# Weights of a hybrid decoder trunk rounded by the loading DMA, and a second convolution buffer

## The chip, the cores and the metric

The kernel runs on one core of a Trainium2 chip. The metric is the device time of one execution in microseconds (us). The core's engines work side by side: PE (TensorE, the matmuls), DVE (VectorE), ACT (ScalarE), POOL (GpSimd) and SP (SyncE, which here only issues DMAs). A DMA is issued by one engine, whose queue it stands in with that engine's other instructions, and is carried out by the core's DMA engines.

## The reference

Two layers (DEPTH = 2) on x of 1024 tokens by 1024 features, all in float32:

```python
for l in range(DEPTH):
    h = rmsnorm(x, norm_mix[l])
    q, k, v, u, ug, ga, gb = split(h @ w_in[l])          # 1024+128+128+512+512+1024+1024 columns
    A = sliding_window_attention(rope(qknorm(q)), rope(qknorm(k)), v, sinks)   # 16 heads, window 128
    a = u * sigmoid(ug)                                   # 512 channels
    y = causal_depthwise_conv(a, conv_w[l], width=31) + conv_b[l]
    B = silu(layernorm(y, over_channels)) @ w_pw[l]       # 512 -> 1024
    x = x + (sigmoid(ga) * A + sigmoid(gb) * B) @ w_out[l]
    x = x + swiglu(rmsnorm(x, norm_ffn[l]))               # 1024 -> 2816 -> 1024
```

## The kernel before

**Layout.** Features lie on the 128 partitions, the 1024 tokens in the free dimension. So a weight tile has 128 rows of the inner dimension and 128 output columns for each of eight row groups: 128x1024 numbers, 512 KB. The convolution's output weights (`wcv`) have four row groups: 128x512, 256 KB.

**A float32 product is three matmuls.** Each operand is split into a high part, which TensorE's rounded float32 type (F32R) holds exactly, and a low part, what is left: w = wh + wl, x = xh + xl. `mm3` issues wh·xh, wh·xl and wl·xh, each as two matmuls of 512 tokens (profile line L253). So one weight tile is used by 48 matmuls (24 for wcv), and its low part is first read by the fifth of them.

**The weights of one layer, in the order of use.** 34 input projections (`win`: first k and v, then conv value and gate, queries and output gates mixed, the order being a list), 8 wcv, 8 output projections (`wout`). They are 50 a layer, 100 in all; the FFN's weights take another path, which the change leaves alone.

**How weights get ready.** `fetch` runs before each weight's use. It starts the load of the weight two ahead and makes the high and low part of the weight one ahead:
- the load: SP issues a DMA into a raw tile (L128, two tiles);
- the high part: ACT casts raw to wh (L136, three tiles);
- the low part, outside the attention stage: POOL subtracts, wl = raw − wh (L143, two tiles). This is so for k and v, the last win, all wcv and all wout, 38 in the two layers;
- the low part, within the attention stage (flag `spaced`): ACT writes wl = −wh (L146), then POOL issues a DMA that reads the weight from memory once more and adds it into wl as it writes (L147, an accumulating DMA). This is so for 62 weights. Here one spare wl tile more goes round, which has the tag "y", that of the convolution's output.

**The attention stage** (66 to 528 us in layer 0, 1386 to 1848 in layer 1) mixes four streams. PE does the projections and, between them, 32 attention units (scores S, L658; transposes L694; values L724). Between score and transpose stand ACT (copy, exponential L678, scaling L685) and DVE (the mask's copy of S into sc, L670); POOL applies band masks (L706, L709). Queries go through rope (POOL L400, L401), a power (POOL L411), and are stored and reloaded (DMA `qs<-q`). The convolution runs on DVE: four chunks of 128 channels, each 31 taps of 128x1024 (the first L514, the others L518, in place on the chunk's tile y). After a chunk's last tap its y is added into the channel sum lsum (ACT copy for the first, L522; POOL add for the others, L524) and stored to memory (SP, L525, DMA `yd<-y`). When all four are done, matmuls with a matrix of means read lsum (L555) for the layer norm, and the chunks are loaded back.

There is **one** y tile (YB = 1), so the next chunk's first tap waits until the store has read it.

**The output stage** (some 528 to 664 us in layer 0) is wcv, where SP also loads two 512 KB gate tiles for each weight, then wout. In wout the residual (L857), the next norm's squares (ACT L301, POOL sum L303) and the first pieces of FFN weights (ACT cast L160, POOL subtraction L162) run beside the matmuls.

**What sets the order.** The order on PE is written by hand throughout, that on DVE in the attention stage and the FFN. The orders on ACT, POOL and SP come from a scheduler that simulates the program's timeline when it is built, so they move when operations come or go. Every engine works through its instructions strictly in order: one that waits holds up all that stand behind it.

Of the kernel before, what the change touches and what calls it, by code (L numbers as in the profile page):

```python
# [12 lines left out]
F32 = mybir.dt.float32  # L13
F32R = mybir.dt.float32r
U32 = mybir.dt.uint32
AF = mybir.ActivationFunctionType
# [36 lines left out]
def trunk(ctx, tc, xT, win, wcv, wout, wgu, wdn, vecs, cosT, sinT, outT):  # L53
# [15 lines left out]
    dp = pool("dp", 1, DRAM)  # L69
    hlp = wp = psm = None  # L70

# [46 lines left out]
    part = [0]  # L118
    spaced = [False]

    spare = []

    def fetch(limit=len(wseq), parts=len(wseq)):
        limit = min(limit, wends[part[0]])
        while given[2] < limit and given[2] <= given[0] + AHEAD + 1:
            src, n = wseq[given[2]]
            raw = wp.tile([P, n], F32, tag="raw", bufs=WRAW, name="raw")
            nc.sync.dma_start(raw, src)  # L128
            raws.append(raw)
            given[2] += 1  # L130
        while given[1] < min(given[2], parts) and given[1] <= given[0] + AHEAD:
            src, n = wseq[given[1]]
            raw = raws.pop(0)
            wh = wp.tile([P, n], F32R, tag="wh", bufs=WHI, name="wh")
            wl = spare.pop() if spare else wp.tile([P, n], F32R, tag="wl", bufs=WLO, name="wl")
            nc.scalar.copy(wh, raw)  # L136
            low(wl, raw, wh, src)
            ready.append((wh, wl))
            given[1] += 1

    def low(wl, raw, wh, src):
        if not spaced[0]:
            nc.gpsimd.tensor_tensor(out=wl, in0=raw, in1=wh.bitcast(F32), op=ALU.subtract)  # L143
            return

        nc.scalar.activation(wl, wh.bitcast(F32), AF.Copy, scale=-1.0)  # L146
        nc.gpsimd.dma_start(wl, src, accum_op=ALU.add)  # L147

# [180 lines left out]
    for l in range(DEPTH):  # L329
# [174 lines left out]
        def conv_taps():  # L504
# [3 lines left out]
            for c in range(CC):  # L508
# [8 lines left out]
                for j in range(1, CW):  # L517
                    nc.vector.scalar_tensor_tensor(out=y, in0=a[:, j:j + T], scalar=V(w0 + j),  # L518
                                                   in1=y, op0=ALU.mult, op1=ALU.add)
                    if j == CW - 1:  # L520
                        if c == 0:
                            nc.scalar.copy(lsum, y)  # L522
                        else:
                            nc.gpsimd.tensor_tensor(out=lsum, in0=lsum, in1=y, op=ALU.add)  # L524
                        nc.sync.dma_start(yd[c], y)  # L525
# [236 lines left out]
        wk = next_w()  # L762
        spaced[0] = True

# [47 lines left out]
        assert conv_done[0] == CC * CW  # L812
        spaced[0] = False
        dve.close()
# [359 lines left out]
TD, AD = 7.5, 5.5  # L1174
YB = 1
S0 = 16
# [11 lines left out]
QSB = 4  # L1188
WRAW, WHI, WLO, T4 = 2, 3, 2, 4
WD, RD = 2, 0  # L1190
# [63 lines left out]
```

## Time and profile before

Three runs took 2641.04, 2643.77 and 2648.74 us; the median is 2643.77. The profiled execution took 2642.97 us, its span is 2641.3 us.

| | |
|---|---|
| busy time in the span | PE 97%, DVE 67%, POOL 53%, ACT 44% |
| mean granted clock of TensorE | 0.992 |
| hardware DMA queue (issued by SP) | 393.63 MB, 44.4% of the DMA engines' time |
| software DMA queue (issued by POOL) | 32.51 MB, 7.3% |
| PE idle in the attention stages | 26.1 us in layer 0, 27.5 us in layer 1 |
| ACT casts wh (L136) | 100, 98.1 us |
| POOL subtractions wl (L143) | 38, 74.3 us |
| ACT wl = −wh (L146) | 62, 65.4 us |
| POOL issues of accumulating DMAs (L147) | 62, 55.1 us |
| POOL additions of channel sums (L524) | 6, 14.8 us |

Rows of the time order have: start (us from the span's start), duration, engine, line, operation, output<-inputs, and in brackets the idle time just before and what ended it. "x2" joins instructions that follow each other. A wait's releaser is the one that came last by the profile.

### The profile page before, as it was taken

To read this page: it belongs to the slowest core of one execution; us is meant where nothing else is said; L and a number is where in the kernel's file an instruction comes from. 1 tells how busy PE (TensorE), PEld (TensorE's weight loads), DVE (VectorE), ACT (ScalarE), POOL (GpSimd) and SP (SyncE) were. 2 spreads that over 40 slices of the span, in tenths; PEclk is the share of its full clock that TensorE was granted. 3 is DMA by queue.
4 is the path that set the end of the run, shared out by engine and by line. 5 is a ranking of instruction groups with operands and counts; after the bars stand their busy time and mean duration, and the time that the engine had idled before them with its cause. 6 is when DMAs were issued, how large, how long until landed. Compare 5 with 4: busy or idle time off the path is not lost.

```text
span 2641.3 us, 33363 instructions
## 1 busy us (share of the span) xinstructions
PE 2554.7 (97%) x11736; PEld 2089.6 (79%) x11736; DVE 1767.1 (67%) x2063; ACT 1161.9 (44%) x2300; POOL 1398.8 (53%) x996
## 2 busy tenths in 40 slices
PE   8998999999999999999999989999999999999999
PEld 6776877888778888878777778778887788888887
DVE  4788997551677777845636989975517777878344
ACT  5465666622522322344534656666325222233443
POOL 3355665325366776755423556543243667777444
PEclk9999999999999999999999999999999999999999
DMA  5444445673345444576634444457733444446666
GB/s 172 100 114 113 93 112 148 221 257 136 120 159 183 152 159 168 198 256 223 216 93 89 114 114 101 121 132 235 258 119 124 170 169 163 148 168 219 213 225 212
DMA packets 146407, 428.35 MB, mean 162 GB/s; under 512 B 17152, under 2 KB 17408, under 8 KB 146240
## 3 DMA queue, kind: packets, MB, share of 16 engines
q1 hardware_dynamic: 137168, 393.63, 44.4%
q0 software_dynamic: 8928, 32.51, 7.3%
q8 instruction: 92, 1.51, 0.2%
q14 instruction: 75, 0.61, 0.1%
q10 hardware_dynamic: 144, 0.09, 0.0%
HBM read 291.68 MB, written 115.34 MB: 154 GB/s over the span
## 4 chain that ended last, share of the span: by engine, by line
PE 36%; DVE 6%; DMA 3%; ACT 2%; POOL 2%; issue 2%; SPq 0%; DVEq 0%; ACTq 0%; POOLq 0%
PE b L879 23%; PE ps L253 10%; DVE y L518 2%; DMA qs<-q 1%; DMA rot<-q 1%; POOL plo L162 1%; DMA yd<-y 0%; PE po L724 0%; PE psv L253 0%; POOL rot L401 0%; ACT wh L136 0%; PE pT L694 0%; DVE q L415 0%; ACT sc L678 0%; POOL q L400 0%
## 5 line engine op out<-in xcount | busy, mean ns | idle before, releaser
L162 POOL TENSOR_TENSOR plo<-fraw,phi 128x512 fp32r<-128x512 f32 x290 | 425.9, 1477 | 232.5 <-ACT phi L160 220.4
L162 POOL TENSOR_TENSOR plo<-fs,phi 128x512 fp32r<-128x512 f32 x160 | 262.3, 1650 | 252.8 <-ACT phi L160 245.2
L160 ACT CAST phi<-fraw 128x512 fp32r<-128x512 f32 x444 | 257.6, 618 | 236.2 <-POOL plo L162 139.7
L518 DVE SCALAR_TENSOR_TENSOR y<-a,vec,y 128x1024 f32<-128x1024 f32 x240 | 355.2, 1480 | 3.8
L253 PE MATMUL ps<-hx,wh 128*128 128x512 f32 x1056 | 340.1, 403 | 7.2 <-ACT hx L294 7.2
L253 PE MATMUL ps<-lx,wh 128*128 128x512 f32 x1056 | 330.5, 394 | 0.8 <-DVE lx L295 0.8
L160 ACT CAST phi<-fs 128x512 fp32r<-128x512 f32 x160 | 95.5, 620 | 533.9 <-DVE fs L175 533.9
L253 PE MATMUL ps<-hx,wl 128*128 128x512 f32 x1056 | 329.4, 393 | 0.0
L162 DVE TENSOR_TENSOR plo<-fraw,phi 128x512 fp32r<-128x512 f32 x154 | 130.5, 853 | 189.7 <-ACT phi L160 187.5
L879 PE MATMUL b<-plo,phi 128*128 128x512 f32 x616 | 240.6, 391 | 3.9 <-DVE plo L162 3.7
L879 PE MATMUL b<-phi,plo 128*128 128x512 f32 x616 | 239.8, 389 | 0.0
L879 PE MATMUL b<-phi 128*128 128x512 f32 x616 | 239.7, 389 | 0.0
L253 PEld LDWEIGHTS ps<-lx,wh 128*128 128x128 f32 x1056 | 200.7, 190 | 45.8 <-DVE lx L295 1.5
L253 PEld LDWEIGHTS ps<-hx,wl 128*128 128x128 f32 x1056 | 200.0, 189 | 43.3
L253 PEld LDWEIGHTS ps<-hx,wh 128*128 128x128 f32 x1056 | 189.6, 191 | 41.7 <-ACT hx L294 7.2
L678 ACT ACTIVATE sc<-sc,nm,fq 128x129 f32<-128x129 f32 x256 | 123.8, 487 | 120.2 <-DVE nm L676 120.0
L143 POOL TENSOR_TENSOR wl<-raw,wh 128x1024 fp32r<-128x1024 f32 (+1 forms) x38 | 74.3, 1957 | 174.7 <-PE ps L253 134.7
L136 ACT CAST wh<-raw 128x1024 fp32r<-128x1024 f32 (+1 forms) x100 | 98.1, 981 | 152.8 <-PE ps L253 121.5
L147 POOL DMA_DIRECT2D wl<-win x62 | 55.1, 888 | 202.6 <-ACT wl L146 198.6
L943 DVE TENSOR_TENSOR g<-g 128x512 f32<-128x512 f32 x88 | 105.4, 1198 | 65.9 <-POOL g L947 46.2
L709 POOL TENSOR_SCALAR_AFFINE_SELECT ph<-ph 128x512 fp32r<-128x512 f32 x64 | 69.8, 1090 | 143.6 <-DVE pl L701 143.6
L947 POOL TENSOR_TENSOR g<-g,u 128x512 f32<-128x512 f32 (+1 forms) x84 | 128.4, 1546 | 30.2 <-DVE u L1000 23.8
(254 smaller groups left out, 6157.6 us busy)
## 6 DMA issues: line engine op xcount, KB each, us to landing
fraw<-wgu SPq DMA_DIRECT2D x88, 512.0 KB
raw<-win SPq DMA_DIRECT2D x68, 512.0 KB
wl<-win POOLq DMA_DIRECT2D x62, 512.0 KB, 6.5
act<-g SPq DMA_DIRECT2D x44, 512.0 KB
dw<-wdn SPq DMA_DIRECT2D x44, 512.0 KB
td<-g SPq DMA_DIRECT2D x44, 512.0 KB
sd<-dw SPq DMA_DIRECT2D x44, 512.0 KB
fraw<-sd SPq DMA_DIRECT2D x88, 256.0 KB
```

The lines of the kernel that those rows point to most:

```text
L136: nc.scalar.copy(wh, raw)
L143: nc.gpsimd.tensor_tensor(out=wl, in0=raw, in1=wh.bitcast(F32), op=ALU.subtract)
L147: nc.gpsimd.dma_start(wl, src, accum_op=ALU.add)
L160: nc.scalar.copy(hi, src)
L162: (eng or nc.gpsimd).tensor_tensor(out=lo, in0=src, in1=hi.bitcast(F32), op=ALU.subtract)
L253: nc.tensor.matmul(ps[:, sl], a[:, wc], b[:, sl], start=first and j == 0, stop=last and j == 2)
L518: nc.vector.scalar_tensor_tensor(out=y, in0=a[:, j:j + T], scalar=V(w0 + j), in1=y, op0=ALU.mult, op1=ALU.add)
L678: nc.scalar.activation(sc[:, n], sc[:, n], AF.Exp, bias=nm[:, n:n + 1], scale=fq[:, 4 * j + n:4 * j + n + 1], accum_out=den[:, n:n + 1])
L709: nc.gpsimd.affine_select(out=src, in_=src.bitcast(F32), pattern=[[0, 4], [-1, P]], compare_op=ALU.is_gt, fill=0.0, base=0, channel_multip ...
L879: nc.tensor.matmul(ps, w[:, ai * P:(ai + 1) * P], x, start=first and j == 0, stop=last and j == 2, skip_group_check=True)
L943: nc.vector.tensor_tensor(out=o, in0=x, in1=y, op=ALU.subtract)
L947: nc.gpsimd.tensor_tensor(out=g[:, sl], in0=g[:, sl], in1=u[:, sl], op=ALU.mult)
```

## The change

Three edits:

1. From the third weight on, there is no raw tile. The load is issued by POOL, straight into the wh tile, with a conversion from F32 to F32R in the DMA (L132 of the changed kernel). It is still started two weights ahead; since it lands in one of the three wh tiles, it waits until PE has finished the weight three before. The low part is always made the second way: ACT wl = −wh, then an accumulating DMA from POOL. So of 100 ACT casts 2 are left, of 38 POOL subtractions 2, ACT's negations become 98 (82 of 128x1024, 16 of 128x512), POOL's accumulating weight DMAs 98, and 98 loads move from SP to POOL. The first two weights of layer 0 keep raw tiles, in a pool of their own.
2. There are two y tiles (YB = 2).
3. A chunk's addition into the channel sum (six in all) is an accumulating DMA issued by POOL, in place of a POOL addition.

```diff
         while given[2] < limit and given[2] <= given[0] + AHEAD + 1:
             src, n = wseq[given[2]]
-            raw = wp.tile([P, n], F32, tag="raw", bufs=WRAW, name="raw")
-            nc.sync.dma_start(raw, src)
+            if given[2] < 2:
+                raw = ip.tile([P, n], F32, name=f"raw{given[2]}")
+                nc.sync.dma_start(raw, src)
+            else:
+
+                raw = wp.tile([P, n], F32R, tag="wh", bufs=WHI, name="wh")
+                nc.gpsimd.dma_start(raw, src)
             raws.append(raw)
...
             raw = raws.pop(0)
-            wh = wp.tile([P, n], F32R, tag="wh", bufs=WHI, name="wh")
             wl = spare.pop() if spare else wp.tile([P, n], F32R, tag="wl", bufs=WLO, name="wl")
-            nc.scalar.copy(wh, raw)
-            low(wl, raw, wh, src)
+            if given[1] < 2:
+                wh = wp.tile([P, n], F32R, tag="wh", bufs=WHI, name="wh")
+                nc.scalar.copy(wh, raw)
+                nc.gpsimd.tensor_tensor(out=wl, in0=raw, in1=wh.bitcast(F32), op=ALU.subtract)
+            else:
+
+                wh = raw
+                nc.scalar.activation(wl, wh.bitcast(F32), AF.Copy, scale=-1.0)
+                nc.gpsimd.dma_start(wl, src, accum_op=ALU.add)
             ready.append((wh, wl))
...
                         if c == 0:
                             nc.scalar.copy(lsum, y)
                         else:
-                            nc.gpsimd.tensor_tensor(out=lsum, in0=lsum, in1=y, op=ALU.add)
+                            nc.gpsimd.dma_start(lsum, y, accum_op=ALU.add)
                         nc.sync.dma_start(yd[c], y)
...
-YB = 1
+YB = 2
...
-WRAW, WHI, WLO, T4 = 2, 3, 2, 4
+WHI, WLO, T4 = 3, 2, 4
```

The scheduler's orders move with it; PE's stays as it is. POOL's order from the end of the attention stage through wcv into wout (layer 0), before; L162 are FFN pieces, L303 the sum of squares:

```order
L143 TENSOR_TENSOR wl<-raw,wh 128x1024
L143 TENSOR_TENSOR wl<-raw,wh 128x512 x8
L143 TENSOR_TENSOR wl<-raw,wh 128x1024 x3
L162 TENSOR_TENSOR plo<-fraw,phi 128x512 x4
L143 TENSOR_TENSOR wl<-raw,wh 128x1024
L303 TENSOR_TENSOR acc<-acc,sq 128x1024
L162 TENSOR_TENSOR plo<-fraw,phi 128x512 x3
L143 TENSOR_TENSOR wl<-raw,wh 128x1024
```

POOL's order at the same place after, from the load of the third wout (lines are two further down in the changed kernel, L164 is L162 before, L305 is L303):

```order
L132 DMA wh<-wout 128x1024
L147 DMA wl<-wout 128x1024
L132 DMA wh<-wout 128x1024
L147 DMA wl<-wout 128x1024
L164 TENSOR_TENSOR plo<-fraw,phi 128x512 x4
L132 DMA wh<-wout 128x1024
L305 TENSOR_TENSOR acc<-acc,sq 128x1024
L164 TENSOR_TENSOR plo<-fraw,phi 128x512 x3
L147 DMA wl<-wout 128x1024
L132 DMA wh<-wout 128x1024
```

Each subtraction has become a load of a later weight and an accumulating DMA; the fourth wout's low part now stands behind a sum of squares and three FFN subtractions, where it stood ahead of them.

ACT's order in the attention stage, before, at a query projection (L605, L607); L678, L685 and L663 belong to attention units:

```order
L136 CAST wh<-raw 128x1024
L605 ACTIVATE q_1388<-ps,vec_95 128x1024
L607 ACTIVATE sqh<-ps 128x1024
L146 ACTIVATE wl<-wh 128x1024
L678 ACTIVATE sc,den<-sc,nm,fq 128x129 x4
L663 COPY sc<-S 128x4x128
```

ACT's order in the same stage after (L680 is L678 before, L631 the query's high part):

```order
L680 ACTIVATE sc,den<-sc,nm,fq 128x129 x4
L631 CAST qhi<-q_1368 128x1024
L146 ACTIVATE wl<-wh 128x1024
L496 ACTIVATE ug<-ug 128x1024
L687 ACTIVATE sc<-sc,ri 128x128 x4
```

The cast is gone, the negation stays.

More of the change, by code (lines that the diff above doesn't have):

```diff
@@ L69, in trunk @@
     dp = pool("dp", 1, DRAM)
-    hlp = wp = psm = None
+    hlp = wp = psm = ip = None
     order = ctx.enter_context(tc.manual_schedule(engines=MAN))
@@ L118, in trunk @@
     part = [0]
-    spaced = [False]
     spare = []
@@ L133, in fetch @@
             raw = raws.pop(0)
-            wh = wp.tile([P, n], F32R, tag="wh", bufs=WHI, name="wh")
             wl = spare.pop() if spare else wp.tile([P, n], F32R, tag="wl", bufs=WLO, name="wl")
-            nc.scalar.copy(wh, raw)
-            low(wl, raw, wh, src)
+            if given[1] < 2:
[6 more added lines that the diff above has]
+                nc.gpsimd.dma_start(wl, src, accum_op=ALU.add)
             ready.append((wh, wl))
             given[1] += 1
[L141 to L147, printed above, removed]
     def next_w():
@@ L762, in trunk @@
         wk = next_w()
-        spaced[0] = True
         spare.append(ap_.tile([P, T], F32R, tag="y", bufs=YB, name="wl"))
@@ L812, in trunk @@
         assert conv_done[0] == CC * CW
-        spaced[0] = False
         dve.close()
```

## The prediction

> **What bounds the kernel now.** I read the page first: busy times, then the chain that ended last.
>
> ```profile
> PE 2554.7 (97%) x11736; PEld 2089.6 (79%) x11736; DVE 1767.1 (67%) x2063; ACT 1161.9 (44%) x2300; POOL 1398.8 (53%) x996
> PE 36%; DVE 6%; DMA 3%; ACT 2%; POOL 2%; issue 2%; SPq 0%; DVEq 0%; ACTq 0%; POOLq 0%
> ```
>
> PE is busy for 97% of 2641.3 us, so the matmuls, which the change leaves alone, are the bound, and about 87 us of idle time are all that can be won, besides clock. The windows (us, then busy time and instructions of PE, PEld, DVE, ACT, POOL, the granted clock, DMA share, GB/s) say where: two in the attention stage of layer 0, then the convolution's pointwise product (wcv).
>
> ```profile
> 198.00:264.00 66.00, 56.63 (x279) 45.53 (x278) 54.05 (x64) 36.89 (x91) 33.28 (x27) 0.95 0.45 113
> 264.00:330.00 66.00, 65.28 (x351) 54.59 (x350) 61.06 (x79) 44.45 (x116) 40.61 (x32) 1.00 0.40 93
> 330.00:396.00 66.00, 60.05 (x299) 48.77 (x298) 59.95 (x73) 40.16 (x101) 41.50 (x31) 0.97 0.47 111
> 540.00:550.00 10.00, 10.00 (x45) 8.03 (x44) 6.31 (x6) 3.34 (x4) 2.15 (x2) 1.00 0.75 223
> ```
>
> The attention stage has gaps (9.4 us in the first window) while DVE is busy for 54 to 61 of 66 us. The output stage has none: whatever makes a weight late there is paid in full. Next, what PE waited for, over the run (total us, times, longest):
>
> ```profile
> PE S L658 <- DMA qs<-q: 14.9, 13, 2.3
> PE S L658 <- DVE sc L670: 13.7, 5, 6.6
> PE pT L694 <- ACT sc L685: 12.6, 15, 2.6
> ```
>
> No wait of PE is for a weight. Two of the 13.7 us have one cause, seen in the time order of DVE (start, duration, then the wait in brackets) and of PE:
>
> ```profile
> 248.42 0.81 DVE L514 TENSOR_SCALAR y<-a,vec 128x1024 f32<-128x1024 f32 x1 [7.93 <-DMA yd<-y]
> 1563.94 0.81 DVE L514 TENSOR_SCALAR y<-a,vec 128x1024 f32<-128x1024 f32 x1 [6.63 <-DMA yd<-y]
> 251.24 0.48 PE L658 MATMUL S<-kh,qs 128*128 128x128 f32 x1 [6.61 <-DVE sc L670]
> 1566.77 0.48 PE L658 MATMUL S<-kh,qs 128*128 128x128 f32 x1 [5.32 <-DVE sc L670]
> ```
>
> The first tap of a channel chunk waits until the one y tile has been stored; DVE's hand-written order holds the mask copy behind it, and PE waits for that copy. Afterwards the clock is down for some us:
>
> ```profile
> 249.00:252.00 3.00, 0.76 (x4) 0.76 (x4) 2.90 (x5) 0.00 (x0) 0.00 (x0) 0.50 0.00 0
> 252.00:255.00 3.00, 3.00 (x11) 2.61 (x11) 2.95 (x5) 2.28 (x9) 2.08 (x3) 0.52 0.00 0
> 1567.00:1570.00 3.00, 3.00 (x12) 2.71 (x13) 2.92 (x6) 2.28 (x9) 1.56 (x3) 0.50 0.00 0
> 1570.00:1573.00 3.00, 3.00 (x10) 2.34 (x9) 2.97 (x4) 2.41 (x4) 1.29 (x2) 0.60 0.19 27
> ```
>
> Busy PE time lost, taken as (1 − clock) × PE's busy time: 0.76 × 0.50 + 3 × 0.48 = 1.8 us, and 3 × 0.50 + 3 × 0.40 = 2.7 us.
>
> **The change, part by part.** (1) **Two y tiles.** A chunk's first tap no longer waits for the store. Direct price: 6.6 + 1.8 + 5.3 + 2.7 = 16.4 us. Part returns: in the windows shown, the one after the stall has only 0.72 us of PE idle time but the next 5.95, so DVE's backlog bites later. I take −14; ends −16.5 and −6 (half of the two stalls, 12/2).
>
> (2) **ACT's 98 casts go.** The chain of waits by line holds them:
>
> ```profile
> by line: PE b L879 22.7%; PE ps L253 10.4%; DVE y L518 2.2%; issue 1.8%; DMA qs<-q 1.2%; DMA rot<-q 0.6%; POOL plo L162 0.5%; DMA yd<-y 0.5%; PE po L724 0.5%; PE psv L253 0.4%; POOL rot L401 0.4%; ACT wh L136 0.4%; PE pT L694 0.3%; DVE q L4
> 1587.29 1.06 ACT wh L136
> 1588.35 1.01 ACT q L605
> ```
>
> 0.4% of 2641.3 is 10.6 us, about ten casts like the one before q. PE also waits for other things there, so I take −7; ends −10.6 and 0.
>
> (3) **POOL's queue in attention.** The accumulating DMAs there now each have a rounding load before them.
>
> ```profile
> L147 POOL DMA_DIRECT2D wl<-win x62: 850/874/1063, 26.4 to 1815.6; - x62
> DMA to landing us min/median/max: 5.2/6.5/9.7
> L147 POOL DMA_DIRECT2D wl<-win x62 | 55.1, 888 | 202.6 <-ACT wl L146 198.6
> ```
>
> About 64 more issues (a rounding load for each weight of the stage, six sums) × 0.87 = 56 us, less than the 198.6 us that POOL already spends before these issues waiting for ACT. A rounding load waits for PE to leave the weight three before, and the masks, rope and query powers stand behind it. POOL is 2% of the chain with 1399 us of work: 56 × (0.02 × 2641.3 / 1399) = 2. I take +2; ends 0 and +6. The channel sums cost nothing: the last add ends 12.45 us before its reader, more than an accumulate's longest landing, 9.7, and POOL saves 2.4 − 0.9 us each.
>
> ```profile
> 432.52 2.38 POOL L524 TENSOR_TENSOR lsum<-lsum,y 128x1024 f32<-128x1024 f32 x1
> 444.97 1.02 PE L555 MATMUL pmu<-lsum,meanmat 128*128 128x512 f32 x2
> ```
>
> (4) **The wcv loop.** Here the POOL subtraction is replaced by a transfer, in a stage without a gap.
>
> ```profile
> 543.55 1.30 POOL L143 TENSOR_TENSOR wl<-raw,wh 128x512 fp32r<-128x512 f32 x1 [4.31 <-ACT wh L136]
> 549.15 1.29 POOL L143 TENSOR_TENSOR wl<-raw,wh 128x512 fp32r<-128x512 f32 x1 [4.30 <-ACT wh L136]
> 544.87 0.33 SPq L128 DMA_DIRECT2D raw<-wcv  x1
> 548.53 0.62 ACT L136 CAST wh<-raw 128x512 fp32r<-128x512 f32 x1 [1.52 <-PE ps L253]
> ```
>
> The period is 5.60 us. When PE leaves a weight at t, one rounding load (0.87) and ACT's negation (0.62) go first, and the accumulate is issued at t + 0.95. Its low part is first read four matmuls after the next period, at t + 5.60 + 0.93 = t + 6.5 (four of 5.60/24). So a landing over 5.55 us stalls PE, by the excess, every weight. At 256 KB nothing was seen. Plain loads: 256 KB in at most 548.53 − 544.87 = 3.7 us; the 512 KB one below in 565.97 − 561.67 = 4.3. An accumulate of 512 KB takes 6.5, that is 2.2 over plain; half to all of that on top of 3.7 is 4.8 to 5.9. Queue load: 0.75 busy now, with one accumulate more. I take a mean excess of 0.15 × 14 weights = +2; ends 0 and, at the longest landing seen, (9.7 − 5.55) × 14 = +58; at 6.5 it is +13.
>
> (5) **The output projection.** Its first low part has to land within the last wcv period but carries 512 KB: issued at t + 1.15 (negation 1.06), landed t + 7.65, wanted t + 6.5: 1.15 in each layer, +2; ends 0 and +8.7 at 9.7. PE begins the first at 576.75 and the third at 598.53 (rows below), 10.89 us each, so later ones fit, except the fourth, which POOL's order puts behind a sum of squares and three subtractions:
>
> ```profile
> 561.67 0.33 SPq L128 DMA_DIRECT2D raw<-wout  x1
> 565.97 1.06 ACT L136 CAST wh<-raw 128x1024 fp32r<-128x1024 f32 x1 [2.16 <-DMA raw<-wout]
> 576.75 0.63 PE L253 MATMUL ps<-hm,wh 128*128 128x512 f32 x2
> 598.53 0.62 PE L253 MATMUL ps<-hm,wh 128*128 128x512 f32 x2
> 599.98 1.06 ACT L301 ACTIVATE sq<-xa 128x1024 f32<-128x1024 f32 x1 [3.27 <-DVE xa L861]
> 600.00 2.40 POOL L143 TENSOR_TENSOR wl<-raw,wh 128x1024 fp32r<-128x1024 f32 x1
> 602.37 2.40 POOL L303 TENSOR_TENSOR acc<-acc,sq 128x1024 f32<-128x1024 f32 x1
> 604.72 3.78 POOL L162 TENSOR_TENSOR plo<-fraw,phi 128x512 fp32r<-128x512 f32 x3
> ```
>
> Without L143, the sum runs 601.0 to 603.4 and the subtractions to 607.2; then the accumulate is issued and lands at 612.4, 613.7 or 616.9. It is wanted at 598.53 + 10.89 + 0.93 = 610.3. Late by 2.1, 3.4 or 6.6: I take +6 for the two layers, a little under the median's 6.8; ends +4 and +13.
>
> Two rules of the Trainium skill bear on this. Page "DMA: Bandwidth & Descriptors", section "Anatomy of one DMA — SWDGE (gpsimd) path", fits such a DMA at about 2.0 us plus bytes over 436 GB/s: 3.2 us for 512 KB. By it parts 4 and 5 vanish and the time would be about 2624, an estimate; this trace's 62 accumulates, 5.2 at the least, disagree, and the measurement decides. Page "SBUF — State Buffer", section "SBUF: two separate sides", says that GpSimd writes the descriptors of DMAs it issues and is locked out while DVE runs a two-port mode, and advises SP or ACT instead. It speaks against this change; that 62 issues stay within 850 to 1063 ns does not show it in the issue, and it is rival C2.
>
> Start and layer boundary: first two weights as before, later subtractions at the boundary lighter: 0. **Sum:** −14 − 7 + 2 + 2 + 2 + 6 = −9 from 2642.97 (0.8 under the median of 2643.77): **2634**.
>
> **Rivals.** B: the DMA load is lighter than its price, nothing is late in parts 4 and 5, and 1 and 2 pay in full: −14 − 7 + 2 = 2624, down to 2618 with both upper ends. For it: the 4.8 end; against: the fourth wout's order. D: attention keeps its length. DVE has 61.06 of 66 us filled in the window after the stall, and casts taken from ACT free nothing for it; 1 and 2 bring −12 together at most, and 3 to 5 (+12) eat it: 2643. For it: the 5.95 us gap that comes back; against: a 7.93 us DVE wait truly goes. C, slower: a 256 KB accumulate behind a rounding load on one queue lands at 7.5 us; from 5.55 on it decides, and (7.5 − 5.55) × 14 = +27 on −9, less the 2 in it, plus 2 more on first wouts: 2661. For it: landings up to 9.7 and a queue at 0.75; against: half the bytes. C2: descriptors held back by DVE's work: one DVE tap of 1.5 us, less 0.3 of cover, makes each wcv landing 1.2 us longer; (0.15 + 1.2) × 14 = 19 instead of 2, minus 5 as DVE is only 6.3 of 10 us busy there: 2646. Against it: those issue times.
>
> **How the numbers follow.** Chances: forecast 0.45, D 0.22, B 0.15, C 0.11, C2 0.07. A measurement can tell 0.3% from no change, 7.9 us: below 2635.8 or above 2651.7. The forecast's own range is 2624 to 2646; six tenths of it, 0.27, count as faster, 0.15 as the same, 0.03 (longer landings) as slower. D splits 0.02, 0.17, 0.03; B is faster, C slower, C2 half and half. Faster: 0.27 + 0.02 + 0.15 = 0.44; slower: 0.03 + 0.03 + 0.11 + 0.04 = 0.21; same 0.35. The range runs from B's low end to short of C's price: 2618 to 2656; what is left out is about 0.05 below and most of C above.
>
> **What would show it.** Right: no wait of the first tap on the y store, none of PE over 4 us near 250 and 1567; two casts in ACT's group; POOL's issues about 0.9 us; a few PE waits under 1 us on wl between 540 and 580 and one of 2 to 4 us near 610. Wrong: PE waiting for wh in attention (rounding loads late), a wl wait every 5.6 us in the wcv stage (C), wl landings whose length follows DVE's load (C2), or attention as long as before although the y wait is gone (D).

## The result: slower by 1.4%

The changed kernel takes 2678.82 us (median of 4 runs, 2673.25 to 2688.41), the kernel before 2643.03 (median of 4). The ratio is 1.0136, with a 95% interval of 1.0098 to 1.0173. The prediction was 2634, range 2618 to 2656: wrong in sign and outside its range. The profiled execution of the changed kernel took 2673.25 us, the fastest of its four, with a span of 2671.5, 30.2 over that of before.

PE's order of matmuls did not move, so each stage can be timed in both traces from the first matmul of a kind to the first of the next. Lengths in us; "start" runs from the execution's start, or from the next layer's first projection, to the first score, and "FFN 1" ends with the last matmul:

| kernel | start 0 | attention 0 | wcv 0 | wout 0 | FFN 0 | start 1 | attention 1 | wcv 1 | wout 1 | FFN 1 |
|---|---|---|---|---|---|---|---|---|---|---|
| before | 101.8 | 430.1 | 44.8 | 87.1 | 662.1 | 91.7 | 431.9 | 44.8 | 87.1 | 656.1 |
| changed | 104.3 | 425.6 | 49.6 | 94.8 | 661.7 | 100.2 | 429.9 | 49.5 | 94.8 | 657.2 |

Of the 30.2 us, 25 come from the two output stages, 11 from the two starts; the attention stages, where the prediction saw a gain of 19, gave 6.5.

### The profile after

The page of the changed kernel: busy time, and the two DMA queues that carry the weights (packets, MB, share of the DMA engines' time):

```profile
PE 2569.4 (96%) x11736; PEld 2103.1 (79%) x11736; DVE 1767.9 (66%) x2063; ACT 1108.7 (41%) x2238; POOL 1401.0 (52%) x1094
q1 hardware_dynamic: 123056, 346.44, 38.0%
q0 software_dynamic: 29088, 97.53, 17.2%
```

ACT has 53 us less to do. POOL's busy time is about the same: some 84 us of subtractions and additions went, and some 94 us of DMA issues, which on POOL count as busy, came. PE's busy time rose by 15 us for the same matmuls: they ran at a lower clock. Some 47 MB went from SP's queue (44.4% before) to POOL's (7.3%); together they take 55.2% of the DMA engines' time for 51.7.

PE's waits in the changed kernel (total us, times, longest):

```profile
PE S L660 <- DMA qs<-q: 18.6, 18, 3.3
PE po L726 <- DVE ssb L411: 15.0, 7, 3.6
PE ps L255 <- DMA wl<-wout: 9.8, 4, 4.3
PE ps L255 <- DMA wl<-wcv: 6.7, 5, 2.7
PE pb L327 <- DVE dg L320: 5.7, 2, 5.2
PE S L660 <- DVE sc L672: 1.4, 2, 0.7
```

The waits of 6.6 and 5.3 us for the mask copy are gone (1.4 us is left of 13.7), as predicted. Four kinds are new or grew by more than 5 us. Two are for low parts of weights (16.5 us), which no matmul waited for before. One is for dg, the product that spreads the norm over the tokens. One is for ssb, the sums of the query norm: 15.0 us with waits of 3.6, where the kernel before had 6.8 us and none over 1.2.

**The output stage.** PE's matmuls in the order of time that waited longest there (layer 0: second wcv, fourth wout; layer 1: fourth wout), then two windows behind the second of them:

```profile
539.37 0.73 PE L255 MATMUL ps<-zh,wl 128*128 128x512 f32 x2 [2.71 <-DMA wl<-wcv]
618.10 1.22 PE L255 MATMUL ps<-hm,wl 128*128 128x512 f32 x2 [3.64 <-DMA wl<-wout]
1955.42 1.22 PE L255 MATMUL ps<-hm,wl 128*128 128x512 f32 x2 [4.31 <-DMA wl<-wout]
```

```profile
618.00:621.00 3.00, 2.90 (x7) 2.33 (x8) 0.00 (x0) 0.00 (x0) 0.39 (x1) 0.50 1.09 310
621.00:624.00 3.00, 3.00 (x9) 2.32 (x8) 0.00 (x0) 0.00 (x0) 0.00 (x0) 0.52 0.32 67
```

After the 3.64 us wait the granted clock is 0.50 and 0.52 for two windows: 2.90 × 0.50 + 3.00 × 0.48 = 2.9 us more. With the first wout's 0.47 that is 7.0 of the 7.7 us by which wout grew in layer 0.

**The start of layer 1.** DVE's row for dg in the changed kernel, then POOL's rows around it, then the same place in the kernel before (DVE, POOL):

```profile
1363.48 5.67 DVE L320 TENSOR_TENSOR dg<-ident,rtok 128x1024 f32<-128x1024 f32 x1 [3.28 <-POOL rtok L315]
1360.86 0.88 POOL L147 DMA_DIRECT2D wl<-win  x1 [2.19 <-ACT wl L146]
1363.11 2.66 POOL L402 TENSOR_TENSOR k<-k,ct 128x1024 f32<-128x1024 f32 x1
1365.42 2.63 POOL L403 TENSOR_TENSOR rot<-rot,st__11109 128x1024 f32<-128x1024 f32 x1
1367.71 1.24 POOL L147 DMA_DIRECT2D wl<-win  x1
```

```profile
1351.80 1.23 DVE L318 TENSOR_TENSOR dg<-ident,rtok 128x1024 f32<-128x1024 f32 x1 [1.72 <-POOL rtok L313]
1352.92 2.38 POOL L400 TENSOR_TENSOR k<-k,ct 128x1024 f32<-128x1024 f32 x1 [1.16 <-DMA rot<-k]
```

The same product took 1.23 us before and 5.67 now. Before, POOL paused 1.16 us for the rotated rows of the keys, and dg ran in the pause. Now POOL went on without one, and dg ended 1.1 us after POOL's second product, about its own length. The pause closed because POOL came later to rtok, the small product that dg reads and that stands ahead of the keys' products on POOL: the accumulating DMA of the first POOL row stood in front of it, having waited 2.19 us for ACT's negation, which itself had waited 2.10 us for the rounding load to land.

**A held tap in attention.** The same in the attention stage, three times (at 371, 1657 and 1708 us). DVE, POOL and PE of the changed kernel at the third:

```profile
1708.27 8.19 DVE L520 SCALAR_TENSOR_TENSOR y<-a,vec,y 128x1024 f32<-128x1024 f32 x2
1716.49 0.17 DVE L411 TENSOR_TENSOR ssb<-pssh,e 128x16 f32<-128x16 f32 x1
1707.88 0.88 POOL L147 DMA_DIRECT2D wl<-win  x1
1708.46 0.96 POOL L711 TENSOR_SCALAR_AFFINE_SELECT pl<-pl 128x512 fp32r<-128x512 f32 x1
1709.23 2.50 POOL L402 TENSOR_TENSOR q<-q,ct 128x1024 f32<-128x1024 f32 x1
1711.55 2.50 POOL L403 TENSOR_TENSOR rot<-rot,st__11109 128x1024 f32<-128x1024 f32 x1
1716.81 1.19 PE L726 MATMUL po<-mo,vv 128*128 128x256 f32 x4 [3.57 <-DVE ssb L411]
```

Two taps took 8.19 us where two take 2.6 (the longest single one 6.9, next fence). POOL issued a DMA and worked through a mask and both rope products of a query without a gap; ssb stood behind the taps, and PE behind ssb. The taps' line of the changed kernel, in ns:

```profile
L520 DVE SCALAR_TENSOR_TENSOR y<-a,vec,y x240: 1255/1285/6898, 71.9 to 1760.8; 128x1024 f32<-128x1024 f32 x120
```

In the kernel before, POOL had a pause ahead of those rope products in 15 of 16 queries, waiting for their rotated rows; in the changed one it waited for them in 8, and six queries have no pause at all (its waits, before and after):

```profile
POOL q L400 <- DMA rot<-q: 29.6, 15, 5.2
```

```profile
POOL q L402 <- DMA rot<-q: 13.2, 8, 2.8
POOL wh L132 <- PE ps L255: 321.0, 60, 16.8
```

A missing pause does not decide it alone: in three of the six queries without one the tap was not held. One of these, DVE and POOL:

```profile
323.72 5.49 DVE L520 SCALAR_TENSOR_TENSOR y<-a,vec,y 128x1024 f32<-128x1024 f32 x2
324.78 3.35 POOL L402 TENSOR_TENSOR q<-q,ct 128x1024 f32<-128x1024 f32 x1
```

In no run did a tap take over 3.6 us where POOL had paused. Why, without a pause, one tap comes in between POOL's instructions and another does not, no run shows.

**What closed the pauses.** ACT and POOL at the seventh query of layer 0, before and then changed:

```profile
369.57 1.06 ACT L136 CAST wh<-raw 128x1024 fp32r<-128x1024 f32 x1
370.52 1.11 ACT L605 ACTIVATE q<-ps,vec 128x1024 f32<-128x1024 f32 x1
372.17 1.56 POOL L709 TENSOR_SCALAR_AFFINE_SELECT ph<-ph 128x512 fp32r<-128x512 f32 x1 [1.99 <-DVE pl L701]
376.52 2.58 POOL L400 TENSOR_TENSOR q<-q,ct 128x1024 f32<-128x1024 f32 x1 [0.74 <-DMA rot<-q]
```

```profile
366.61 1.12 ACT L607 ACTIVATE q<-ps,vec 128x1024 f32<-128x1024 f32 x1
369.16 1.55 POOL L711 TENSOR_SCALAR_AFFINE_SELECT ph<-ph 128x512 fp32r<-128x512 f32 x1 [1.47 <-DVE pl L703]
372.57 2.54 POOL L402 TENSOR_TENSOR q<-q,ct 128x1024 f32<-128x1024 f32 x1
```

POOL does not come late to these products. In both kernels it stands idle for DVE ahead of the first mask, and from that mask to the product it works for 3.6 us before and 3.4 us now. It is q that comes early. ACT writes it 1.65 us ahead of the mask before and 2.55 us now, since the cast that stood in front of it is gone; so the rotated rows are there when POOL has done its masks. In the kernel before, a cast stands directly ahead of q in all 16 queries, in the changed kernel in none.

The page "SBUF — State Buffer" of the Trainium skill, section "Who interferes with whom", says that a DVE instruction with two SBUF inputs contends with a GpSimd instruction that reads SBUF, and that the one that comes second blocks until the other has finished. The taps and dg have two such inputs. dg, which starts 0.37 us after the keys' first product, agrees; the tap at 1708.27 starts 0.19 us ahead of the mask by the profile and was held all the same. What the page does not say, and 6.9 and 5.67 us show, is that DVE was held for several instructions of POOL that followed each other at once.

### The profile page after: what moved, and what is told of

Read it like the earlier page. It is cut to its first block, busy times and chain, and to the rows that moved or that the text cites. A ratio compares the mean times of both kernels' runs of the same rounds, so it can differ in the third digit from the quotient of the medians.

```text
span 2671.5 us, 33275 instructions
## 1 busy us (share of the span) xinstructions
PE 2569.4 (96%) x11736; PEld 2103.1 (79%) x11736; DVE 1767.9 (66%) x2063; ACT 1108.7 (41%) x2238; POOL 1401.0 (52%) x1094
## 4 chain that ended last, share of the span: by engine, by line
PE 65%; DVE 11%; DMA 10%; issue 7%; POOL 4%; ACT 2%; SPq 1%; DVEq 0%; POOLq 0%; ACTq 0%
PE b L879 42%; PE ps L255 18%; DMA qs<-q 4%; DVE y L520 4%; DMA fraw<-wgu 2%; PE po L726 1%; DMA fraw<-act 1%; PE S L660 1%; PE pT L696 1%; PE S L661 1%; POOL rot L403 1%; POOL wl L147 1%; DMA rot<-q 1%; ACT sc L680 1%; DMA wl<-wout 1%
## 5 line engine op out<-in xcount | busy, mean ns | idle before, releaser
L164 POOL TENSOR_TENSOR plo<-fraw,phi 128x512 fp32r<-128x512 f32 x290 | 420.8, 1461 | 234.2 <-ACT phi L162 221.8
L164 POOL TENSOR_TENSOR plo<-fs,phi 128x512 fp32r<-128x512 f32 x160 | 264.5, 1664 | 252.9 <-ACT phi L162 238.8
L520 DVE SCALAR_TENSOR_TENSOR y<-a,vec,y 128x1024 f32<-128x1024 f32 x240 | 375.4, 1564 | 3.9
L162 ACT CAST phi<-fraw 128x512 fp32r<-128x512 f32 x444 | 257.1, 618 | 249.6 <-POOL plo L164 135.9
L162 ACT CAST phi<-fs 128x512 fp32r<-128x512 f32 x160 | 95.5, 620 | 533.6 <-DVE fs L177 519.8
L164 DVE TENSOR_TENSOR plo<-fraw,phi 128x512 fp32r<-128x512 f32 x154 | 128.4, 839 | 192.1 <-ACT phi L162 190.0
L146 ACT ACTIVATE wl<-wh 128x1024 fp32r<-128x1024 f32 (+1 forms) x98 | 96.9, 989 | 176.0 <-PE ps L255 165.4
L680 ACT ACTIVATE sc<-sc,nm,fq 128x129 f32<-128x129 f32 x256 | 123.7, 486 | 92.0 <-DVE nm L678 91.5
L879 PEld LDWEIGHTS b<-plo,phi 128*128 128x128 f32 x616 | 115.6, 188 | 31.3 <-DVE plo L164 7.2
L879 PEld LDWEIGHTS b<-phi 128*128 128x128 f32 x616 | 115.6, 188 | 24.6 <-ACT phi L162 0.4
L879 PEld LDWEIGHTS b<-phi,plo 128*128 128x128 f32 x616 | 115.6, 188 | 23.6
```

Source lines behind the costliest of these rows:

```text
L162: nc.scalar.copy(hi, src)
L164: (eng or nc.gpsimd).tensor_tensor(out=lo, in0=src, in1=hi.bitcast(F32), op=ALU.subtract)
L680: nc.scalar.activation(sc[:, n], sc[:, n], AF.Exp, bias=nm[:, n:n + 1], scale=fq[:, 4 * j + n:4 * j + n + 1], accum_out=den[:, n:n + 1])
L879: nc.tensor.matmul(ps, w[:, ai * P:(ai + 1) * P], x, start=first and j == 0, stop=last and j == 2, skip_group_check=True)
```

## The experiments

e1 to e5 start from the changed kernel, the others from e5 or e9, as named. Ratios are to the kernel before on the same chip, where its medians were 2646 to 2648 us. Stage lengths of all runs:

| run | start 0 | attention 0 | wcv 0 | wout 0 | FFN 0 | start 1 | attention 1 | wcv 1 | wout 1 | FFN 1 | ratio (95% interval) |
|---|---|---|---|---|---|---|---|---|---|---|---|
| e1 | 115.2 | 429.4 | 44.8 | 87.0 | 661.0 | 100.8 | 427.1 | 44.9 | 87.0 | 656.2 | 1.0057 (1.0035, 1.0078) |
| e2 | 115.7 | 440.7 | 51.2 | 95.4 | 665.6 | 99.8 | 446.6 | 51.6 | 93.1 | 657.2 | 1.0218 (1.0176, 1.0259) |
| e3 | 104.7 | 429.0 | 49.5 | 95.2 | 662.8 | 92.7 | 435.7 | 51.9 | 94.4 | 657.2 | 1.0116 (1.0092, 1.0139) |
| e4 | 111.3 | 434.7 | 50.0 | 91.3 | 660.6 | 98.0 | 433.2 | 49.5 | 91.5 | 657.6 | 1.0155 (1.0129, 1.0180) |
| e5 | 105.1 | 429.6 | 44.8 | 87.1 | 661.1 | 93.8 | 431.1 | 44.8 | 87.1 | 655.6 | 1.0002 (0.9989, 1.0016) |
| e6 | 104.5 | 431.5 | 44.8 | 87.1 | 665.9 | 94.4 | 434.0 | 44.8 | 87.1 | 655.8 | 1.0034 (1.0020, 1.0047) |
| e7 | 105.0 | 431.6 | 44.8 | 87.1 | 659.8 | 93.6 | 434.9 | 44.8 | 87.0 | 656.3 | 1.0017 (1.0003, 1.0030) |
| e8 | 109.1 | 478.2 | 44.8 | 87.1 | 660.4 | 98.0 | 470.5 | 44.8 | 87.1 | 657.1 | 1.0349 (1.0329, 1.0369) |
| e9 | 102.1 | 422.3 | 44.8 | 87.0 | 659.7 | 91.2 | 424.4 | 44.8 | 87.1 | 657.0 | 0.9929 (0.9914, 0.9944) |
| e10 | 104.4 | 443.2 | 44.8 | 87.0 | 661.9 | 93.4 | 441.3 | 44.8 | 87.1 | 656.8 | 1.0109 (1.0096, 1.0123) |
| e11 | 103.0 | 429.3 | 44.8 | 87.1 | 667.6 | 91.8 | 433.6 | 44.8 | 87.1 | 658.6 | 1.0009 (0.9992, 1.0025) |
| e12 | 101.7 | 430.2 | 44.8 | 87.1 | 660.0 | 91.2 | 429.9 | 45.3 | 87.1 | 655.5 | 0.9968 (0.9956, 0.9980) |

An attention stage is not the same in every execution: in the changed kernel, e3 and e4, which are alike there, it took 425.6, 429.0 and 434.7 us in layer 0 and 429.9, 435.7 and 433.2 in layer 1. Differences of under 5 us in one stage of one trace are therefore not read as effects.

### e1: the output stages' weights take the old path

```diff
+    plain = lambda i: i % 50 >= 34
...
             if given[2] < 2:
                 raw = ip.tile([P, n], F32, name=f"raw{given[2]}")
                 nc.sync.dma_start(raw, src)
+            elif plain(given[2]):
+                raw = rp[0].tile([P, n], F32, tag="raw", bufs=2, name="raw")
+                nc.sync.dma_start(raw, src)
             else:
...
-            if given[1] < 2:
+            if given[1] < 2 or plain(given[1]):
                 wh = wp.tile([P, n], F32R, tag="wh", bufs=WHI, name="wh")
```

The raw tiles lie in a pool that opens once the attention stage's memory is free.

> The changed kernel, but the 16 convolution-output and 16 output-projection weights take the old path (SP loads a raw tile, ACT casts, POOL subtracts); input projections, y tiles and channel sums as changed. Theory 1 (the output stage's 25 us come from low parts that are transferred where they were computed): both output stages go back to the length of before, 131.9 us, and the time falls by 20 to 28 us against the changed kernel, to about 2652. Rival (the transfers only fill a lag that the attention stage leaves behind, or the DMA queues stay full of gate, residual and FFN loads anyway): under 8 us come back and PE still waits in the output stage, now for raw tiles or casts.

2659.46 us. Both output stages are back to the length of before (131.8 and 131.9 us against 131.9 and 131.9), where the changed kernel took 144.4 and 144.3. The rival falls: all 25 us are the price of getting these 32 weights ready through POOL's DMAs, and the waits seen there are for their low parts. The whole time fell by about 20 us only, since in this profile dg was held in both layers (the starts took 115.2 and 100.8 us).

### e2: one y tile

```diff
-YB = 2
+YB = 1
```

> The changed kernel with one y tile again. Theory 1 (the second tile is worth what the prediction priced, its gain being hidden by new waits of another origin): the two waits of 5 to 7 us of the scores for DVE come back near 250 and 1580 with the low clock behind them, and the time rises by 10 to 16 us against the changed kernel. Rival (rival D of the prediction: the attention stage is bound by DVE and keeps its length): within 4 us of the changed kernel.

2706.68 us. The attention stages are 15.1 and 16.7 us longer than the changed kernel's, and the long waits for the mask copy are back:

```profile
PE S L660 <- DVE sc L672: 15.6, 4, 8.5
```

The traces' 31.8 us compare the slowest of e2's four executions with the fastest of the changed kernel's; by the ratios (1.0218 against 1.0136) the tile is worth 22 us. The size is over the expectation, the direction right: the second tile was worth its price, and rival D, in which it is worth nothing, falls. What was unexpected is the comparison with the kernel before. It has one y tile too, and its attention stages were 10.6 and 14.7 us shorter than these. So something else in the change costs the attention stage about as much as the y tile gives.

### e3: the keys' rope products on DVE

```diff
-            after(1 if l else NA + 0.5, lambda: rope(k32))
+            after(1 if l else NA + 0.5, lambda: rope(k32, 0, nc.vector))
```

Here `rope` takes the engine of its two products as a third argument.

> The changed kernel, with the two rope products of the keys on DVE and not on POOL, in both layers. Theory 1 (at the start of layer 1 the 1.23 us product dg on DVE took 5.67 us because POOL ran two products at that time): dg takes 1.2 to 1.3 us in both layers, PE's wait of 5.2 us for it goes, the time falls by 5 to 9 us. Rival (dg was held by something else, such as the DMA that POOL issues there): dg stays above 3 us and the time stays within 3 us; or two more products on DVE cost 2.5 us there.

2676.57 us. DVE's rows for dg in the two layers:

```profile
38.90 1.23 DVE L320 TENSOR_TENSOR dg<-ident,rtok 128x1024 f32<-128x1024 f32 x1 [3.13 <-POOL rtok L315]
1368.40 1.23 DVE L320 TENSOR_TENSOR dg<-ident,rtok 128x1024 f32<-128x1024 f32 x1 [3.06 <-POOL rtok L315]
```

With no product on POOL beside it, dg takes 1.23 us, and the start of layer 1 went from 100.2 to 92.7 us (before: 91.7). In e1 and e2 dg took 5.67 us in layer 0 as well, and their first starts are 11 us longer. So whether it is held changes from trace to trace, at 7 to 11 us a time with the low clock behind it. In the ratio (1.0116 against 1.0136) the repair can't be told from noise; the rows show it.

### e4: early FFN low parts on DVE

```diff
                     for c in (c0, c1):
-                        yield piece(r[:, c])
+                        yield piece(r[:, c], eng=nc.vector)
```

> The changed kernel, with the low parts of the first eight FFN weight pieces of each layer on DVE and not on POOL, so that in the output projection the fourth weight's accumulating DMA stands behind the sum of squares alone. Theory 1 (the place in POOL's queue makes PE wait there, 3.6 and 4.3 us, and the low clock after it costs 2 to 3 us more): issued 3.7 us earlier it lands in time, both waits fall under 1 us, the time falls by 9 to 14 us. Rival (the landing is late because the DMA engines are 96 to 105% busy there): PE's wait for the fourth low part stays above 2 us, and the time falls by less than 4 us.

2686.55 us. In wout of layer 0 two waits are left, for the third and the fourth low part:

```profile
620.99 0.73 PE L255 MATMUL ps<-hm,wl 128*128 128x512 f32 x2 [1.06 <-DMA wl<-wout]
633.68 0.73 PE L255 MATMUL ps<-hm,wl 128*128 128x512 f32 x2 [1.49 <-DMA wl<-wout]
```

In layer 1 the fourth cost 2.73 us. The wout stages took 91.3 and 91.5 us against 94.8 and 94.8: 6.8 of the 15.4 us came back, under the expected 9 to 14. Both theories hold in part: the place in POOL's queue made the wait long, and with the place mended the transfer, in a stage where the DMA engines are 94 to 105% busy, is still late; whether that load makes it late was not tested. The whole time did not fall, since dg was held in both layers (5.66 and 3.37 us).

### e5: e1 and e3 together

> The changed kernel with the old path for the output stages' weights and the keys' rope products on DVE. Theory 1 (the two losses lie in different places): both come back, and the time is 10 to 25 us under that of the old path alone, so between 3 us under and 5 us over the kernel before; from the layer's start to the first score as before within 4 us. Rival (the start's loss moves to another instruction that POOL holds up): less than 5 us under the old path alone.

2646.91 us, ratio 1.0002 (0.9989 to 1.0016): the same as the kernel before, 13 us under the old path alone. The output stages are as before, the starts 2 to 3 us over. So outside the attention stages all but these 5 us of the loss is found. In them two y tiles still bring nothing (429.6 and 431.1 us against 430.1 and 431.9). The next runs start from this kernel.

### e6: four wh tiles

```diff
-WHI, WLO, T4 = 3, 2, 4
+WHI, WLO, T4 = 4, 2, 4
```

> As the run with both repairs, with four wh tiles in place of three, so that a rounding load waits for a weight that PE has long left. Theory 1 (rounding loads that wait for PE at the head of POOL's queue hold up the masks and rope behind them and make the attention stage slow): POOL's 321 us of idle time before these loads fall below 60, each attention stage gets 3 to 10 us shorter. Rival (they hold up nothing that is wanted soon; the loss lies in DVE and POOL keeping each other out): attention within 2 us of the run with both repairs.

2655.74 us. Attention took 431.5 and 434.0 us, no shorter. But the edit did not do what it was for: POOL still stood idle for 149.6 us before the rounding loads, waiting for PE, where e5's was 140.8. The run says that a fourth tile doesn't help; it does not test whether such waits cost anything.

### e7: channel sums by POOL again

```diff
-                            nc.gpsimd.dma_start(lsum, y, accum_op=ALU.add)
+                            nc.gpsimd.tensor_tensor(out=lsum, in0=lsum, in1=y, op=ALU.add)
```

> As the run with both repairs, with the channel sums as POOL additions again. The prediction put the accumulating DMA at nothing, with 1.5 us of POOL saved each: then each attention stage stays within 2 us. Rival (the accumulating DMA of an SBUF tile into an SBUF tile, which POOL issues, is what keeps DVE or a y tile waiting): attention 3 to 8 us shorter in each layer.

2650.96 us, ratio 1.0017. Attention is 2.0 and 3.8 us longer, which one trace cannot tell from its spread; the rival, a loss by the accumulating DMA, falls. One thing more: in layer 1 of this run no tap took over 3.4 us, and yet the stage is 3.8 us longer than e5's, in which two taps were held. So the held taps alone do not make the stages long.

### e8: the queries' first rope product on DVE

```diff
-            (after if later else now)(later, lambda: eng.tensor_tensor(out=src, in0=src, in1=ct, op=ALU.mult))
+            (after if later else now)(later, lambda: nc.vector.tensor_tensor(out=src, in0=src, in1=ct, op=ALU.mult))
```

> As the run with both repairs, with the first rope product of the queries on DVE (16 more DVE operations of about 1.2 us), so that POOL never runs two long products in a row. Theory 1 (a DVE tap that starts beside such a row is held until its end, 6.9 us for 1.3, and the norm's sum ssb behind it makes PE wait 3.6 us): no tap over 4 us, no wait of PE for ssb over 2 us. If these holds set the stage's length, each attention stage gets 3 to 8 us shorter; rival (DVE is the bound and gets 10 us more work in each layer): 3 to 10 us longer, though the holds go.

2739.28 us, attention 48.6 and 39.4 us longer than e5's. No tap took over 3.42 us, so the holds went as expected. But the product on DVE now waits for the rotated rows, in the order written by hand, with everything behind it:

```profile
DVE q L407 <- DMA rot<-q: 129.1, 16, 10.8
```

The loss is this wait, not the work. The run tells nothing of what the holds cost.

### e9: SP loads and ACT casts in attention too

```diff
-                raw = wp.tile([P, n], F32R, tag="wh", bufs=WHI, name="wh")
-                nc.gpsimd.dma_start(raw, src)
+                raw = wp.tile([P, n], F32, tag="raw", bufs=1, name="raw")
+                nc.sync.dma_start(raw, src)
...
-                wh = raw
+                wh = wp.tile([P, n], F32R, tag="wh", bufs=WHI, name="wh")
+                nc.scalar.copy(wh, raw)
                 nc.scalar.activation(wl, wh.bitcast(F32), AF.Copy, scale=-1.0)
                 nc.gpsimd.dma_start(wl, src, accum_op=ALU.add)
```

The loop also makes the next weight's parts ahead of the load behind it, so that one raw tile will do.

> As the run with both repairs (two y tiles, channel sums by accumulating DMA), but in the attention stage too the weights are loaded by SP into a raw tile (one tile there, two in the output stage) and cast by ACT, as before the change; the low parts come by negation and accumulating DMA as in both kernels. So of the change the second y tile and the sums are left. Theory 1 (the rounding loads cost the attention stage what the second y tile gives it, 12 to 14 us a layer): each attention stage 8 to 14 us shorter than in the run with both repairs, the time 2620 to 2632 us. Rival (the attention stage is bound by DVE, and its length does not depend on who loads): attention within 3 us, the time 2640 to 2652. A second rival: the casts on ACT and the single raw tile cost more than the rounding loads did, attention 3 to 10 us longer.

2625.99 us, ratio 0.9929 (0.9914 to 0.9944): faster than both kernels, by 21 us than the kernel before and by 21 than e5. Attention took 422.3 and 424.4 us, 7.3 and 6.7 under e5's. That is a little under the 8 to 14 expected; the rest came from the starts (3.0 and 2.6). The total lies in the forecast, and both rivals fall. PE's idle time makes 5.9 of the 14.0 us between the attention stages of e5 and e9, the rest is its lower clock in e5. In e9 a cast stands directly ahead of q again in all 16 queries.

### e10: the query norm's sums earlier

```diff
-QN = 5
+QN = 3
```

This one starts from e5 again.

> As the run with both repairs, with the query norm's sums (PE) and ssb (DVE) two steps earlier in the hand-written order, so that ssb stands ahead of the two taps of which POOL's rope products hold one. Theory 1 (held taps cost PE only through ssb behind them): PE's waits of up to 3.6 us for ssb go, 5 and 10 us of gaps in the two layers, and each attention stage gets 4 to 10 us shorter, clock included. Rival (what is behind the held tap is late anyway, the mask copy next): the waits for ssb go and waits for the mask copy or for sc take their place, attention within 3 us.

2676.26 us. PE's waits:

```profile
PE pssh L413 <- ACT sc L685: 13.7, 8, 1.8
PE po L731 <- POOL pl L716: 12.6, 2, 6.3
```

The waits for ssb went and others took their place, and attention took 13.6 and 10.2 us more than in e5, against both expectations. The taps held for 6.9 us are still there, three of them. But the eight waits of the sums for ACT come from the edit itself, which asks for the sums earlier; so the run does not price what stands behind a held tap.

### e11: small rounding DMAs beside SP's loads

From e9, in the load branch:

```diff
                     raw = wp.tile([P, n], F32, tag="raw", bufs=1, name="raw")
+                    whs[given[2]] = wp.tile([P, n], F32R, tag="wh", bufs=WHI, name="wh")
+                    nc.gpsimd.dma_start(whs[given[2]][:, 0:32], src[:, 0:32])
                 nc.sync.dma_start(raw, src)
```

> As the run with SP's loads, but before ACT casts an attention weight into wh, POOL issues a rounding DMA of its first 32 columns (16 KB) into the same tile, with the same wait for PE as the changed kernel's rounding load; ACT's cast then overwrites them. So POOL's queue gets the loads' issues and waits, without their traffic and without taking ACT's casts away. Theory 1 (the rounding loads cost the attention stage by standing in POOL's queue): each attention stage 4 to 8 us longer than with SP's loads, and POOL starts the queries' rope products without a pause in at least 4 of 16 cases, with a tap held over 4 us. Rival (the cost lies in the transfers or in what moves when the casts go): attention within 2 us, no tap over 4 us.

2651.48 us, ratio 1.0009. Attention is 7.0 and 9.2 us longer than e9's, and as long as e5's. FFN of layer 0 took 7.9 us more, which the edit does not touch and which stays unexplained. The waits of POOL for the rotated rows, and of PE for ssb, in e9 and then in e11:

```profile
POOL q L405 <- DMA rot<-q: 21.4, 15, 2.8
PE po L729 <- DVE ssb L414: 6.5, 7, 1.2
```

```profile
POOL q L410 <- DMA rot<-q: 14.1, 7, 2.7
PE po L734 <- DVE ssb L419: 27.1, 10, 3.6
```

With SP's loads POOL waits ahead of the rope products in 15 of 16 cases and the longest tap takes 3.5 us. With DMAs of 16 KB in POOL's queue it waits in 7, taps are held for up to 6.9 us, and PE waits 20 us more for ssb (and 7 less for qs). So the loss does not need the traffic of the loads, and the expectation's numbers came, but for 9.2 us where 8 was the most. But its cause is not shown by this run, because the edit moved ACT's order too. The cast now waits for the small DMA (28.0 us in 15 waits), and the scheduler put it elsewhere. ACT and POOL at the seventh query of layer 0:

```profile
359.69 1.12 ACT L615 ACTIVATE q<-ps,vec 128x1024 f32<-128x1024 f32 x1
362.24 1.54 POOL L719 TENSOR_SCALAR_AFFINE_SELECT ph<-ph 128x512 fp32r<-128x512 f32 x1 [1.47 <-DVE pl L711]
362.56 1.04 ACT L135 CAST wh<-raw 128x1024 fp32r<-128x1024 f32 x1
```

The cast stands behind q, q again comes 2.55 us ahead of the mask (1.63 in e9), and POOL again stands idle for DVE before it. By these rows the pauses closed because q came early, as in the changed kernel, and not because POOL came late. No run has the loads on POOL and q at its old time, so the two are not separated by experiment.

### e12: e9 with one y tile

```diff
-YB = 2
+YB = 1
```

> As the run with SP's loads, with one y tile. Of the change only the channel sums by accumulating DMA are left (and one raw tile for two in the attention stage). Theory 1 (the second tile is worth the direct price of the two waits, 16.4 us for both layers, and little comes back later): the waits for the y store return, each attention stage 6 to 10 us longer than with two. Rival (the gain of the run with SP's loads is the channel sums', the y tile's being given back behind the stall): under 4 us longer in each layer.

2640.66 us, 14.7 over e9. Attention is 7.9 and 5.5 us longer, and the long waits are back:

```profile
PE S L663 <- DVE sc L675: 17.3, 3, 8.6
```

So with the loads on SP the second y tile is worth 13.4 us of attention, close to the direct price. The ratio of e12, 0.9968, leaves some 8 us to the other edits it keeps, which no single stage shows; its attention stages are those of before within 2 us.

## Why the prediction was wrong

**What bounds the kernel**: right. PE's idle time and clock hold all of the difference, and the output stage paid every late weight in full.

**Step 1, the y tile, −14**: right, 13.4 us by e9 and e12. The stall went, and little of it came back. In the changed kernel the tile was worth more (22 us by e2's ratio, 31.8 by its trace).

**Steps 2 and 3, casts gone and POOL's queue, −7 and +2**: this is the step that failed worst, in sign. By e5 against e9 the loading by POOL, casts included, costs the attention stages 14.0 us.

The casts' term is the one that the rows contradict. The prediction let q come a cast earlier and counted that as gain, with 0 as the worst end. The cast did hold q up by 0.9 us. But this is what made POOL pause ahead of the rope products, and without it pauses closed, taps were held, and PE waited longer for ssb. Where POOL had paused, a tap came in between the two products, at 3.2 to 3.3 us. This chain is read from rows and not isolated by a run, and the holds are not all of the 14 us (e7).

The queue's term compared 56 us of new issues with the 198.6 us that POOL waited for ACT elsewhere. But idle time in sum is no cover for an instruction in one place, as rtok at the start of layer 1 shows.

Both terms also rest on a misreading of the chain that ended last. Its shares in the page add up to 51% of the span, because it goes back only to 1292 us. So 0.4% for the casts and 2% for POOL are layer 1's alone; taken for both layers, they would have put the forecast further off.

The prediction named DVE holding up POOL (rival C2); it was POOL that held up DVE. The trace of before showed that such holding happens, in the view of the taps' line (min, median and longest ns):

```profile
L518 DVE SCALAR_TENSOR_TENSOR y<-a,vec,y x240: 1252/1285/3284, 71.1 to 1740.8; 128x1024 f32<-128x1024 f32 x120
```

The longest, of 3.2 to 3.3 us, each ran beside a rope product. The sum held no row of it.

**Step 3, channel sums, 0**: no loss was found (e7). The cover of 12.45 us runs from the add's start; from its end to its reader are 10.1 us, still more than 9.7.

**Step 4, wcv, +2**: mechanism right, size off: 9.5 us by the stages. The excess was taken as a mean over 14 weights. In fact the landing was in time for most, and most of the wait fell on the second weight of each stage (2.71 and 2.32 us), when the gate tiles are loaded ahead. The landing medians, in the view of DMA issues, were within the estimate of 4.8 to 5.9 for 256 KB:

```profile
wl<-wcv POOLq DMA_DIRECT2D x16, 256.0 KB, 5.5
wl<-wout POOLq DMA_DIRECT2D x16, 512.0 KB, 7.7
```

**Step 5, wout, +8**: mechanism right, size off. The fourth low part was 3.64 and 4.31 us late (worked out: 2.1, 3.4 or 6.6), the first 0.47 and 1.41 (1.15). But the stages grew by 15.4 us. The low clock after a wait, which had been added to the y stall's price, was left out here; in layer 0 it was 2.9 us. By e4 under half of the 15.4 depends on the place in POOL's queue.

**Starts, 0**: wrong, +11.0 us in the profile, 8.5 of it at layer 1, for dg held by the keys' rope products (e3). The 2.5 at layer 0, where dg was not held in this trace, are also in e3 and e5 and not in e9; what makes them was not found.

The sum stood at −9. With the measured sizes it is −13.4 + 14.0 + 9.5 + 15.4 + 11.0 = +36.5, against +30.2 in the profile and +35.8 in the medians. The difference to the profile lies in the attention stages, where the sum has +0.6 and the profile −6.5. Rival B falls by the output stages. D had the attention stage's outcome nearly right, but not its cause: e12 and e9 show that the y tile does bring its price there. C asked for late landings at every wcv weight; only the second of each stage was as late (issued at 531.10, read at 539.37 in layer 0). The slower side had 0.21, for reasons of which only the late low parts came true.

## What to carry to other kernels

Work moved to an engine with idle time is not free if that engine keeps another out while it runs: look for the pauses in which the other gets through, and for what makes them; here it was an instruction of a third engine, and the change removed it. Where a stage has no gap, a part computed on chip in 1.3 to 2.4 us is not to be exchanged for a transfer that lands in 5 to 8 us unless it is issued a whole period earlier. And PE's waits are to be priced with the low clock that can follow them, everywhere in the sum: in the changed kernel's trace it fell to 0.50 after every wait of 3.3 us or more but the first of the execution, and stayed at 1.00 after the 2.71 us wait in wcv.

## What the runs showed of the hardware that was not expected

- A DVE product of 1.23 us took 5.67, and a tap of 1.29 took 6.9, while POOL ran several instructions on SBUF tiles one after the other. With a pause of POOL of under a microsecond before them, or POOL's products elsewhere, they did not; without a pause they did in about half of the cases (3 of 6 queries in the changed kernel, 5 of 8 in e11).
- With some 64 DMAs of 16 KB, issued by POOL, two attention stages were 16 us longer. ACT's casts moved with them, so how much is POOL's queue stays open.
- After PE's wait of 3.64 us in an otherwise full stage, the granted clock was 0.50 to 0.52 for about 6 us: 2.9 us lost behind a wait of 3.6.
